# The first stage of layer 0 in a new order: vectors by rows, biases by columns, blocks finished pair by pair

## The chip, the cores and the metric

The kernel runs on one core of a Trainium2 chip. The metric is the time of one execution in device microseconds. The time before is the median of three runs, 1631.57 us (1629.46 to 1635.71).

## The reference, cut to what matters

One step of a trunk of two layers over 1024 latent tokens and 128 context tokens of width 1024, in float32. The change touches the start of layer 0: the modulation vectors, the pre-norm and the projection to keys and values.

```python
def adaln(cond, w, b):                       # w: 1024 x 3072
    m = (jax.nn.silu(cond) @ w + b)[:, None, :]
    return split_last(m, (D_MODEL, D_MODEL, D_MODEL))
def pre_norm(x, g, mod):
    shift, scale, _ = mod
    return rms_norm(x, g) * (1 + scale) + shift
...
for layer in range(DEPTH):
    mod_p = adaln(c_ctx[None, :], w_mod[layer], b_mod[layer])   # context tokens
    mod_s = adaln(c, w_mod[layer], b_mod[layer])                # latent tokens
    hp = pre_norm(xp, g_pre[layer], mod_p)
    hs = pre_norm(xs, g_pre[layer], mod_s)
    # layer 0: q, k, v, gates and the pooling input are columns of h @ w_in_e
```

## The kernel before

**Tokens and blocks.** The nine token tiles (eight latent, one context) of 128 x 1024 are `xn[t]`; group g is tiles 3g to 3g+2. Width 1024 is cut into eight blocks k of 128. `hTh[k]` and `hTl[k]` hold block k of the normed, scaled and shifted tokens, transposed, as a high part and a rest; weights are split in the same way into `whi` and `wlo`, and one product is three matmuls (high by high, high by rest, rest by high).

**The steps.** `norm_x(t)` squares and sums a tile on ACT (`sqx`), takes the root on ACT (`xd`), the reciprocal on DVE (`xr`) and scales the tile on DVE. `pn(k, g)` is `prenorm_k`: three transposes on PE into a PSUM tile `tp`, scale and shift on DVE into `hf` (two buffers), the high part on ACT (`hTh`), the rest on POOL (`hTl`, which frees `hf`). `kvg(k, ts)` does the nine matmuls per three token tiles that add block k to the key and value sums in five PSUM banks `acc`. A key and value chunk of 512 KB (`raw`) serves four blocks; `kv.split` makes its `whi` on ACT and its `wlo` on DVE.

**Modulation in quarters.** `mod_block(kp)` computes a quarter of shift and scale (two blocks k) for both conditions: 32 small matmuls of `wmb` (four loads of 512 KB) against `silrep`, the SiLU of the condition vectors spread over 32 rows; then `mrow` is written by DVE, and `mod_block_end` transposes it on PE and writes `sh` and `sc` on DVE. `pn(k, .)` needs quarter k // 2. `mod_ss(1)` does the same for layer 1 later, beside the query products.

**Order.** The program sets the order of every engine's instructions by hand; each engine and SP's queue, which issues all loads, works in that order. PE's order before: quarter 0, `pn(0..1, 0)`, the products of those, quarter 1, and from then on products of blocks prepared one or more steps earlier, between them the `pn` of later blocks and groups; group 2 follows late. Each quarter's end is issued after products of earlier blocks. Buffers: weights, squares and small tables share 17 tiles `w`; five PSUM banks `B` hold two of `acc`, the modulation and `tp`.

**Vectors before.** `c`, `c_ctx` and `g_pre` are loaded straight into columns (four bytes at a time), the bias `b_mod` of each quarter as rows spread over 32 partitions (`bm0`), added to `mrow`. Five matmuls of zeros open the sums in `acc` (L569).

**What follows.** At the end of the stage the first half of the query weights is split (`wl.need(0)`: twice `whi` on ACT, `wlo` on DVE), the rotary tables are scaled on POOL (`rtq`, `rtk`), and the query products (`qkv`) run beside the norm and transposition of the keys (`kv1` to `kv4`).

Of the kernel before, what the change touches and what calls it, by code (L numbers as in the profile page):

```python
# [19 lines left out]
EPS = 1e-6  # L20
# [35 lines left out]
class Kern:  # L56
# [87 lines left out]
    def setup0(self):  # L144
        nc, I = self.nc, self.I
        ct = self.K([128, 8, 2], name="ct")
        self.dma(ct[:, :, 0], I["c"][0].rearrange("(k p) -> p k", p=128))
        self.dma(ct[:, :, 1], I["c_ctx"].rearrange("(k p) -> p k", p=128))
        sl = self.K([128, 8, 2], name="sl")
        nc.scalar.activation(out=sl, in_=ct, func=AF.Silu)  # L150
        self.silrep = self.K([128, 8, 16, 2], name="silrep")
        self.vcopy(self.silrep, sl[:, :, None, :].to_broadcast([128, 8, 16, 2]))

    def setup(self):
        nc, I = self.nc, self.I
        self.ident = self.K([128, 128], name="ident")
        self.dma(self.ident, I["k_ident"])
        self.gpre = self.K([128, 2, 8], name="gpre")
        self.dma(self.gpre, I["g_pre"].rearrange("l (k p) -> p l k", p=128))
        self.eps = self.K([128, 1], name="eps")  # L160
        nc.vector.memset(self.eps, EPS)
        self.ones = self.K([128, 32], name="ones")
        nc.vector.memset(self.ones, 1.0)
# [19 lines left out]
    def mod_block_load(self, kp):  # L183

        r = []
        for i in range(2):
            for h in range(2):
                t = self.W([128, 4, 256], name="wmb")
                c = 1024 * i + 256 * kp
                self.dma(t, self.I["w_mod"][0, 512 * h:512 * h + 512, c:c + 256].rearrange("(k p) c -> p k c", p=128))  # L190
                r.append(t)
        return r

    def mod_block(self, kp, wt):

        ps = self.C("modps")
        for k in range(8):
            for j in range(4):
                self.mm(ps[32 * j:32 * j + 32, 0:128], self.sil(k),
                        wt[2 * (j // 2) + k // 4][:, k % 4, 128 * (j % 2):128 * (j % 2) + 128], k == 0, k == 7)  # L200
# [12 lines left out]
    def mod_ss(self, l):  # L213
# [18 lines left out]
        def fin():  # L232
            ps = box["ps"]
            bm = self.W([128, 512], name="bm")
            self.bcast_rows(bm, I["b_mod"][l], 512)
            mrow = self.W([128, 512], name="mrow")
            self.vtt(mrow, ps, bm, ALU.add)
            box["m"] = mrow

        def fin2():  # L240
            mrow = box["m"]
            ps2 = self.C("modT").rearrange("p (i q) -> p i q", i=4)
            for i in range(4):
                self.tr(ps2[:, i, :], mrow[:, 128 * i:128 * i + 128])
            v = ps2.rearrange("p i (j r) -> p i j r", j=4)
            self.vcopy(self.sh[l].rearrange("p (j i) s -> p i j s", j=2), v[:, :, 0:2, 0:2])
            self.vts(self.sc[l].rearrange("p (j i) s -> p i j s", j=2), v[:, :, 2:4, 0:2], 1.0, op0=ALU.add)
            self.vtt(self.sc[l], self.sc[l], self.gpre[:, l, :, None].to_broadcast([128, 8, 2]))
# [57 lines left out]
    def prenorm_k(self, l, g, k, xn, hi, lo, veng=False):  # L306

        b = self.B("tp")
        for i in range(3):
            self.tr(b[:, 128 * i:128 * i + 128], xn[i][:, 128 * k:128 * k + 128])  # L310
        hf = self.T([128, 384], tag="hf")
# [213 lines left out]
def layer0(kn):  # L525
# [18 lines left out]
    mb = {}  # L544
    mb[0] = kn.mod_block_load(0)
    load_x(0)
    kn.setup()
    kn.bm0 = kn.W([128, 4, 128], name="bm0")
    src = I["b_mod"][0]
    for j in range(4):  # L550
        kn.dma(kn.bm0[32 * j:32 * j + 32], bass.AP(tensor=src.tensor, offset=src.offset + 1024 * (j // 2) + 128 * (j % 2),
                                                   ap=[[0, 32], [256, 4], [1, 128]]))
    for t in range(1, 3):
        load_x(t)
    kv.load()
    for t in range(3, 6):
        load_x(t)
    mb[1] = kn.mod_block_load(1)
    for t in range(6, 9):
        load_x(t)  # L560

# [4 lines left out]

    zero = kn.W([128, 512], F32R, name="zero")
    nc.vector.memset(f32(zero), 0.0)
    for i in range(5):  # L569
        kn.mm(acc[i], zero[:, 0:128], zero, True, False)  # L570
# [4 lines left out]
    def pn(k, g):  # L575
        c = slice(384 * g, 384 * g + 384)
        kn.prenorm_k(0, g, k, xn[3 * g:3 * g + 3], hTh[k][:, c], hTl[k][:, c])
# [9 lines left out]
    kn.mod_block_end(*kn.mod_block(0, mb.pop(0)))  # L587
    for t in range(3):
        norm_x(t)
    pn(0, 0)  # L590
    mb[2] = kn.mod_block_load(2)
    pn(1, 0)
    kv.split(True)
    for t in range(3, 6):
        norm_x(t)
    for k in range(2):
        kvg(k, range(3))
    for k in range(2):
        pn(k, 1)
    m1 = kn.mod_block(1, mb.pop(1))  # L600
    mb[3] = kn.mod_block_load(3)
    kvg(0, range(3, 6))
    kn.mod_block_end(*m1)
    for k in range(2, 4):
        pn(k, 0)
    kvg(1, range(3, 6))
    for k in range(2, 4):
        pn(k, 1)
    for t in range(6, 9):
        norm_x(t)  # L610
    kvg(2, range(0, 6))
    m2 = kn.mod_block(2, mb.pop(2))
    kvg(3, range(0, 6))
    kn.mod_block_end(*m2)
    for k in range(2):
        pn(k, 2)
# [17 lines left out]
    wl._load(0)  # L634
    for k in range(2, 4):
        pn(k, 2)
    for k in range(4):
        pn(4 + k // 2, k % 2)
        kvg(k, range(6, 9))
    pn(4, 2)  # L640
    pn(5, 2)
    m3 = kn.mod_block(3, mb.pop(3))
    kvg(4, range(9))
    kn.mod_block_end(*m3)
    for g in range(3):
        pn(6, g)
    kvg(5, range(9))
    for g in range(3):
        pn(7, g)
    for c, w in rt.values():  # L650
        for i in range(2):
            kn.ptt(c[:, i], cs[:, i], w[:, i, None, :].to_broadcast([128, 8, 64]))
    wl.need(0)
    wl._load(1)
    kvg(6, range(9))
    kvg(7, range(9))
# [1642 lines left out]
```

## Time and profile before

| | us |
|---|---|
| median of three runs | 1631.57 |
| the profiled execution | 1633.59 |
| its span, first to last instruction | 1631.8 |
| PE busy, share of the span | 1542.5, 95% |
| mean granted clock of PE | 0.979 |
| start to the first key and value product | 25.09 |
| that product to the first query product | 47.88 |

The profiled execution is 2.0 us longer than the median, and 1.8 longer than its own span. PE's busy time is counted with the tails of pipelined matmuls. The page's lines by source often show one line for all matmuls (L97) or copies (L113, L118), since helpers issue them; the names of the tiles tell them apart.

### The profile page before, as it was taken

How to read it: one execution, taken by the hardware profiler on the slowest of the kernel's cores; microseconds unless marked ns; L12 is line 12 of the kernel's file. 1: busy time of each engine (PE TensorE's matmuls, PEld its weight loads, DVE VectorE, ACT ScalarE, POOL GpSimd, SP SyncE). 2: the span in 40 equal slices, each digit the busy share in tenths (PEclk: the TensorE clock that was granted, in tenths of full speed). 3: DMA queues.
4: the chain of work that ended last, by engine and by line, in shares of the span. 5: the costliest groups of instructions: out<-in, count | busy, mean ns of one | idle time of the engine just before them, and what ended most of it. 6: DMA issues, size and time to landing. Idle time of an engine off the chain costs nothing.

```text
span 1631.8 us, 23732 instructions
## 1 busy us (share of the span) xinstructions
PE 1542.5 (95%) x9132; PEld 1232.0 (76%) x9132; DVE 847.1 (52%) x1838; ACT 649.9 (40%) x1370; POOL 610.4 (37%) x485
## 2 busy tenths in 40 slices
PE   5989999999899999999999999999999999999998
PEld 4978998945455588898989898999865566655686
DVE  3574333347767555534354444424775665657633
ACT  4431211255455433445454544443453343444311
POOL 1643212058658423641303113001155454546421
PEclk7999999999999999999999999999999999999999
DMA  9443104120001132410404131040000000013341
GB/s 304 127 175 100 40 27 143 38 104 14 1 13 40 65 104 78 86 36 14 96 16 80 31 74 38 20 146 9 15 4 25 9 26 15 20 46 96 110 143 52
DMA packets 118805, 105.33 MB, mean 65 GB/s; under 512 B 45924, under 2 KB 104548, under 8 KB 118692
## 3 DMA queue, kind: packets, MB, share of 16 engines
q1 hardware_dynamic: 118692, 103.81, 21.5%
q8 instruction: 72, 1.18, 0.3%
q14 instruction: 41, 0.34, 0.1%
HBM read 88.05 MB, written 15.75 MB: 64 GB/s over the span
## 4 chain that ended last, share of the span: by engine, by line
PE 78%; DVE 8%; ACT 3%; POOL 2%; issue 1%; DMA 0%; SPq 0%; DVEq 0%; POOLq 0%; ACTq 0%
PE cg L97 15%; PE yps L97 11%; PE st L97 9%; PE gate L97 8%; PE pv L97 8%; PE mp L97 5%; PE lat L97 4%; PE cpv L97 3%; PE cS L97 2%; PE cT L106 2%; PE dq L97 2%; PE qkv L97 2%; DVE ms L131 1%; DVE mx L933 1%; PE dk L97 1%
## 5 line engine op out<-in xcount | busy, mean ns | idle before, releaser
L124 POOL TENSOR_TENSOR acc<-acc,P 128x1024 f32<-128x1024 f32 x98 | 233.3, 2381 | 109.9 <-ACT P L969 106.3
L969 ACT ACTIVATE P<-st 128x512 f32<-128x512 f32 x288 | 167.7, 597 | 189.8 <-PE st L97 170.7
L933 DVE TENSOR_REDUCE mx<-mp 128x1 f32<-128x384 f32 x384 | 193.1, 549 | 93.6 <-PE mp L97 91.0
L124 POOL TENSOR_TENSOR wlo<-raw,whi 128x1024 fp32r<-128x1024 f32 x36 | 87.3, 2427 | 275.6 <-ACT whi L113 220.0
L97 PE MATMUL yps<-whi,ohl 128*128 128x512 f32 x576 | 183.4, 393 | 0.0
L97 PE MATMUL cg<-hT1h,whi 128*128 128x384 f32 x480 | 170.9, 356 | 1.8 <-DVE hf L133 1.2
L97 PE MATMUL cg<-hT1h,wlo 128*128 128x384 f32 x480 | 163.8, 341 | 1.9 <-POOL wlo L124 1.9
L97 PE MATMUL cg<-hT1l,whi 128*128 128x384 f32 x480 | 163.4, 340 | 0.0
L97 PEld LDWEIGHTS yps<-whi,ohl 128*128 128x128 f32 x576 | 108.2, 188 | 26.0 <-issue 2.4
L97 PE MATMUL yps<-wlo,ohl 128*128 128x512 f32 x288 | 112.2, 390 | 0.0
L97 PE MATMUL gate<-hTh,whi 128*128 128x384 f32 x288 | 98.8, 343 | 4.8 <-ACT whi L113 4.8
L97 PE MATMUL gate<-hTh,wlo 128*128 128x384 f32 x288 | 97.5, 339 | 1.3 <-DVE wlo L121 1.3
L97 PE MATMUL gate<-hTl,whi 128*128 128x384 f32 x288 | 97.3, 338 | 0.0
L97 PEld LDWEIGHTS cg<-hT1h,whi 128*128 128x128 f32 x480 | 91.6, 191 | 6.6 <-issue 3.3
L97 PEld LDWEIGHTS cg<-hT1h,wlo 128*128 128x128 f32 x480 | 91.5, 191 | 2.2 <-POOL wlo L124 2.2
L97 PEld LDWEIGHTS cg<-hT1l,whi 128*128 128x128 f32 x480 | 91.7, 191 | 0.5
L1541 ACT ACTIVATE cs<-cs,cnm 128x640 f32<-128x640 f32 (+1 forms) x64 | 54.8, 857 | 92.0 <-DVE cnm L131 91.1
L97 PE MATMUL pv<-P,dV 128*64 128x512 f32 x288 | 80.0, 636 | 0.0
L97 PE MATMUL pv<-P,V 128*64 128x512 f32 x288 | 79.2, 628 | 0.0
L113 ACT CAST whi<-raw 128x1024 fp32r<-128x1024 f32 (+2 forms) x60 | 61.8, 1038 | 22.5 <-DMA raw<-in_w_in_e 8.7
L124 POOL TENSOR_TENSOR acc<-P 128x1024 f32<-128x1024 f32 x14 | 33.4, 2382 | 92.5 <-ACT P L969 91.9
L97 PEld LDWEIGHTS mp<-KH,QP 128*128 128x128 f32 x192 | 33.7, 190 | 41.7 <-DVE mx L933 14.7
(417 smaller groups left out, 3563.8 us busy)
## 6 DMA issues: line engine op xcount, KB each, us to landing
raw<-in_w_in_o SPq DMA_DIRECT2D x20, 512.0 KB, 4.0
raw<-in_w_in_e SPq DMA_DIRECT2D x18, 512.0 KB, 6.9
wmb<-in_w_mod SPq DMA_DIRECT2D x16, 512.0 KB, 9.1
wm<-in_w_mod SPq DMA_DIRECT2D x16, 512.0 KB, 5.5
wg<-in_w_mod SPq DMA_DIRECT2D x16, 512.0 KB, 4.0
x<-xr SPq DMA_DIRECT2D x9, 512.0 KB, 2.6
xr<-x SPq DMA_DIRECT2D x9, 512.0 KB, 3.9
xn<-in_x_sample SPq DMA_DIRECT2D x8, 512.0 KB, 8.0
```

The source lines that it names most:

```text
L97: self.nc.tensor.matmul(out=out, lhsT=l, rhs=r, start=st, stop=sp)
L106: self.nc.tensor.transpose(out, in_, self.ident[0:n, 0:n])
L113: self.nc.scalar.copy(out=out, in_=in_)
L124: self.nc.gpsimd.tensor_tensor(out=out, in0=a, in1=b, op=op)
L131: self.nc.vector.tensor_scalar(out=out, in0=a, scalar1=s1, scalar2=None, op0=op0)
L933: kn.nc.vector.tensor_reduce(out=self.mx[:, h, t, c:c + 1], in_=b, axis=AX.X, op=ALU.max)
L969: kn.nc.scalar.activation(out=P[:, h], in_=a, func=AF.Exp, scale=self.scale)
L1541: nc.scalar.activation(out=s[:, 0:n], in_=s[:, 0:n], func=AF.Exp, bias=nm, accum_out=sm)
```

## The change

- **Vectors.** `c`, `c_ctx`, `g_pre` and both layers' shift and scale biases are loaded as 64 rows of 128 by five transfers, and the identity by one, all six issued from ACT's queue ahead of ACT's other work. One transpose on PE turns the rows into columns; SiLU reads the PSUM tile, one DVE copy keeps the rest, and 1 is added to the scale biases once. `eps` and `ones` are set by POOL.
- **Biases.** `mrow` becomes a copy, and the biases are added to the columns at the end. For layer 1 the load of broadcast bias rows goes, the copy of `mrow` is on ACT.
- **Loads.** SP begins with x tiles 0 to 2, then quarter 0, the first half of the key and value weights, x 3 to 5, the second half, x 6 to 8, quarter 1. Quarters are loaded in the order in which their halves are used.
- **Zeros.** 25 matmuls of zeros instead of five before quarter 0, and five more behind its end.
- **Order.** Pairs of blocks are finished one after the other: for each group g the products `kvg(k, g)` alternate with `pn(k, g + 1)`; the next quarter's block stands between groups 1 and 2, its end behind group 2, and then the next pair's `pn(k, 0)`.

```diff
     def setup0(self):
...
+        self.ident = self.K([128, 128], name="ident")
+        nc.scalar.dma_start(out=self.ident, in_=I["k_ident"])
+        rows = self.rows = self.T([64, 128], tag="rows", bufs=1)
+        rv = lambda a: a.rearrange("(k p) -> k p", p=128)
+        for r, a in ((0, I["c"][0]), (8, I["c_ctx"]), (32, I["b_mod"][0, 0:2048]), (48, I["b_mod"][1, 0:2048])):
+            nc.scalar.dma_start(out=rows[r:r + a.shape[0] // 128], in_=rv(a))
+        nc.scalar.dma_start(out=rows[16:32], in_=I["g_pre"].rearrange("l (k p) -> (l k) p", p=128))
+
+    def setup(self):
+        nc = self.nc
+        b = self.B("col")[:, 0:64]
+        self.tr(b, self.rows)
+        sl = self.T([128, 2, 8], tag="sl", bufs=1)
+        nc.scalar.activation(out=sl, in_=b[:, 0:16].rearrange("p (s k) -> p s k", s=2), func=AF.Silu)
         self.silrep = self.K([128, 8, 16, 2], name="silrep")
+        self.vcopy(self.silrep, sl.rearrange("p s k -> p k s")[:, :, None, :].to_broadcast([128, 8, 16, 2]))
+        cols = self.K([128, 48], name="cols")
+        self.vcopy(cols, b[:, 16:64])
...
+        self.vts(self.bmc[:, :, 1], self.bmc[:, :, 1], 1.0, op0=ALU.add)
...
-        self.vtt(mrow, ps[:, 0:128], self.bm0[:, kp, :], ALU.add)
+        self.vcopy(mrow, ps[:, 0:128])
...
-        self.vcopy(self.sh[0][:, ks, :], v[:, 0:2, 0:2])
-        self.vts(self.sc[0][:, ks, :], v[:, 2:4, 0:2], 1.0, op0=ALU.add)
+        bc = lambda i: self.bmc[:, 0, i, ks, None].to_broadcast([128, 2, 2])
+        self.vtt(self.sh[0][:, ks, :], v[:, 0:2, 0:2], bc(0), ALU.add)
+        self.vtt(self.sc[0][:, ks, :], v[:, 2:4, 0:2], bc(1), ALU.add)
...
+    G = [range(3), range(3, 6), range(6, 9)]
+    zeros(10)
+    kn.setup()
+    zeros(10)
+    zeros(5, True, False)
+    m = kn.mod_block(0, mb.pop(0))
     for t in range(3):
         norm_x(t)
+    tps = [kn.prenorm_t(k, xn[0:3]) for k in range(2)]
+    kn.mod_block_end(*m)
+    zeros(5, False, False)
+    for k in range(2):
+        pn(k, 0, tps[k])
+    kv.split1(0, True)
     mb[2] = kn.mod_block_load(2)
+    for g in range(3):
+        if g < 2:
+            for t in G[g + 1]:
+                norm_x(t)
+        for k in range(2):
+            kvg(k, G[g])
+            if g < 2:
+                pn(k, g + 1)
+        if g == 0:
+            kv.split1(1, True)
+    m = kn.mod_block(1, mb.pop(1))
     mb[3] = kn.mod_block_load(3)
...
+    kn.mod_block_end(*m)
     for k in range(2, 4):
+        pn(k, 0)
+    for q in range(1, 4):
+        for g in range(3):
+            for k in range(2 * q, 2 * q + 2):
+                kvg(k, G[g])
+                if g < 2:
+                    pn(k, g + 1)
+            if g == 1 and q < 3:
+                m = kn.mod_block(q + 1, mb.pop(q + 1))
+            if g == 1 and q == 3:
...
+                wl.need(0)
+                wl._load(1)
+            if g == 2 and q < 3:
+                kn.mod_block_end(*m)
+                for k in range(2 * q + 2, 2 * q + 4):
+                    pn(k, 0)
```

More of the change, by code (lines that the diff above doesn't have):

```diff
@@ L145, in setup0 @@
         nc, I = self.nc, self.I
[L146 to L150, printed above, removed]
-        self.silrep = self.K([128, 8, 16, 2], name="silrep")
[L152 to L163, printed above, removed]
+        self.eps = self.K([128, 1], name="eps")
@@ L183, in mod_block_load @@
     def mod_block_load(self, kp):
[L185 to L188, printed above, removed]
+        r = {}
+        for h in range(2):
+            for i in range(2):
+                t = r[i, h] = self.W([128, 4, 256], name="wmb")
                 c = 1024 * i + 256 * kp
                 self.dma(t, self.I["w_mod"][0, 512 * h:512 * h + 512, c:c + 256].rearrange("(k p) c -> p k c", p=128))
-                r.append(t)
         return r
@@ L233, in fin @@
             ps = box["ps"]
-            bm = self.W([128, 512], name="bm")
-            self.bcast_rows(bm, I["b_mod"][l], 512)
             mrow = self.W([128, 512], name="mrow")
-            self.vtt(mrow, ps, bm, ALU.add)
+            self.acopy(mrow, ps)
             box["m"] = mrow
@@ L245, in fin2 @@
             v = ps2.rearrange("p i (j r) -> p i j r", j=4)
-            self.vcopy(self.sh[l].rearrange("p (j i) s -> p i j s", j=2), v[:, :, 0:2, 0:2])
-            self.vts(self.sc[l].rearrange("p (j i) s -> p i j s", j=2), v[:, :, 2:4, 0:2], 1.0, op0=ALU.add)
+            for x, (d, j) in enumerate(((self.sh, 0), (self.sc, 2))):
+                bc = self.bmc[:, l, x].rearrange("p (j i) -> p i j", j=2)[:, :, :, None].to_broadcast([128, 4, 2, 2])
+                self.vtt(d[l].rearrange("p (j i) s -> p i j s", j=2), v[:, :, j:j + 2, 0:2], bc, ALU.add)
             self.vtt(self.sc[l], self.sc[l], self.gpre[:, l, :, None].to_broadcast([128, 8, 2]))
@@ L310, in prenorm_k @@
             self.tr(b[:, 128 * i:128 * i + 128], xn[i][:, 128 * k:128 * k + 128])
+        return b
+    def prenorm_k(self, l, g, k, xn, hi, lo, veng=False, b=None):
+        if b is None:
+            b = self.prenorm_t(k, xn)
         hf = self.T([128, 384], tag="hf")
@@ L544, in layer0 @@
     mb = {}
+    for t in range(3):
+        load_x(t)
     mb[0] = kn.mod_block_load(0)
[L546 to L555, printed above, removed]
+    kv.load1(0)
     for t in range(3, 6):
         load_x(t)
-    mb[1] = kn.mod_block_load(1)
+    kv.load1(1)
     for t in range(6, 9):
         load_x(t)
+    mb[1] = kn.mod_block_load(1)
     hTh = [kn.S([128, 1152], F32R, name=f"hTh{k}") for k in range(8)]
@@ L568, in layer0, with zeros, pn @@
     nc.vector.memset(f32(zero), 0.0)
-    for i in range(5):
-        kn.mm(acc[i], zero[:, 0:128], zero, True, False)
+    def zeros(n, st=True, sp=True):
+        for i in range(n):
+            kn.mm(acc[i % 5], zero[:, 0:128], zero, st, sp)
     def kvps(t):
         return acc[t // 2][:, 256 * (t % 2):256 * (t % 2) + 256]
-    def pn(k, g):
+    def pn(k, g, b=None):
         c = slice(384 * g, 384 * g + 384)
-        kn.prenorm_k(0, g, k, xn[3 * g:3 * g + 3], hTh[k][:, c], hTl[k][:, c])
+        kn.prenorm_k(0, g, k, xn[3 * g:3 * g + 3], hTh[k][:, c], hTl[k][:, c], b=b)
     def kvg(k, ts):
@@ L634, in layer0 @@
     wl._load(0)
+    kn.mod_block_end(*m)
     for k in range(2, 4):
[L636 to L656, printed above, removed]
+        pn(k, 0)
[8 more added lines that the diff above has]
+            if g == 1 and q == 3:
+                for c, w in rt.values():
+                    for i in range(2):
+                        kn.ptt(c[:, i], cs[:, i], w[:, i, None, :].to_broadcast([128, 8, 64]))
+                wl.need(0)
[4 more added lines that the diff above has]
+                    pn(k, 0)
     p1.__exit__(None, None, None)
```

35 lines of the change are left out of this document (7 added, 28 removed).

## The prediction

> **What bounds the kernel now.** I read the page's span first, then a table of stretches, then the timeline of the stretch that the change touches, then the waits behind it.
>
> ```profile
> span 1631.8 us, 23732 instructions
> ```
>
> The change rewrites what lies between the start and the first query product. These rows give that stage in three parts, and three short stretches beside them; the columns are the stretch, its length, the busy time of PE, PEld, DVE, ACT and POOL, the granted clock, the share of the DMA engines and GB/s.
>
> ```profile
> 0.00:25.09 25.09, 8.80 (x77) 5.67 (x77) 5.51 (x17) 9.03 (x16) 1.78 (x6) 0.81 0.87 266
> 25.09:46.14 21.05, 18.88 (x219) 16.59 (x220) 12.83 (x25) 12.00 (x25) 6.32 (x7) 0.82 1.08 361
> 46.14:72.97 26.83, 25.69 (x259) 24.35 (x259) 15.18 (x33) 10.39 (x19) 17.92 (x17) 1.00 0.45 124
> ```
> ```profile
> 5.00:10.00 5.00, 3.56 (x21) 2.14 (x25) 0.83 (x4) 0.34 (x2) 0.00 (x0) 1.00 1.10 362
> 16.00:32.00 16.00, 8.41 (x31) 6.29 (x31) 10.23 (x21) 9.71 (x19) 1.96 (x2) 0.50 1.06 375
> ...
> 91.00:94.00 3.00, 3.00 (x16) 3.00 (x15) 1.38 (x6) 0.32 (x2) 2.18 (x4) 0.50 0.00 0
> ```
>
> Up to 25.09 us PE has little to do: the first quarter of the modulation waits for its bias rows and its transposed result for the norms. Then PE is 90% busy, at half clock until about 32 us; from 46.14 it is 96% busy (25.69 of 26.83) at full clock. So the last part is bound by PE itself, and only the first 25 us and the half clock are there to be won. Whatever makes the last part wait is a loss.
>
> ```profile
> 1.87 2.47 SPq L109 DMA_DIRECT2D wmb<-in_w_mod  x4
> ...
> 3.84 1.28 ACT L150 ACT_TABLE_LOAD   x1 [3.84 <-DMA ct<-in_c_ctx]
> ...
> 5.38 0.29 DVE L118 COPY silrep<-sl 128x256 f32<-128x256 f32 x1 [5.38 <-ACT sl L150]
> ...
> 16.56 0.29 DVE L121 TENSOR_TENSOR mrow<-modps,bm 128x128 f32<-128x128 f32 x1 [10.30 <-DMA bm<-in_b_mod]
> ...
> 20.90 0.75 DVE L131 TENSOR_SCALAR xn<-xn,xr 128x1024 f32<-128x1024 f32 x1
> ...
> 23.99 1.99 ACT L113 CAST whi<-raw 128x1024 fp32r<-128x1024 f32 x2
> ...
> 25.09 0.58 PE L97 MATMUL kv<-whi,hTh 128*128 128x256 f32 x1 [2.26 <-ACT whi L113]
> ```
>
> **The front, up to the first product.** The bias rows leave the path: the add at 16.56, which sat 10.30 us for them, becomes a copy. What binds next is the weights of quarter 0. Three x tiles and four weight tiles, 3.67 MB, now go first; SP's first issue moves from the small vectors to x, data runs from about 2.2 us (before, the weights issued at 1.87 were flowing by 4), and at 362 GB/s the last lands at 12.3. The rest of the block and the copy: 13.4. DVE is in order, so the reciprocals and scalings of the three norms stand behind that copy: 3 x 0.92 = 2.8, 16.2. Transposes, scale and shift, two hf (0.68 each), two hTh and the first whi (1.0, half of the pair of 1.99) on ACT follow: the first product at 20.6 instead of 25.09. That is a gain of 4.5 us.
>
> **The first section (blocks k = 0 and 1).** Order on each engine decides here. ACT gets three norms right behind that whi, and PE's transposes for group 1 stand ahead of kvg(1, group 0).
>
> ```profile
> 40.69 1.05 ACT L302 ACTIVATE sqx<-xn 128x1024 f32<-128x1024 f32 x1
> ...
> 42.07 1.04 ACT L302 ACTIVATE sqx<-xn 128x1024 f32<-128x1024 f32 x1
> ...
> 45.13 0.75 DVE L131 TENSOR_SCALAR xn<-xn,xr 128x1024 f32<-128x1024 f32 x1
> ```
>
> A norm takes 42.07 - 40.69 = 1.38 of ACT, three take 4.1, and the last xn ends 1.05 after that (45.88, against a last square that began at 43.45 and would be over with 1.38 at 44.83). So x 3 to 5 are ready at 20.6 + 4.1 + 1.05 = 25.7; PE, which ran kvg(0, group 0) by 23, waits 2.7. Then nine products 1.1 and the transposes, the hTh of (1, group 1) at 28.6, whi of the second half 29.6, three more norms 33.8, their xn 34.8, kvg(1, group 1) until 35.9, the chain of (1, group 2) to its hTl 3.1, seven products 0.85: 39.9. Quarter 1 of the modulation (1.9) follows bare, its copy and transpose (0.4) too: 42.2.
>
> **The steady part.** Now each pair of blocks is finished alone: kvg and pn alternate, and the next pair's first transposes come only after the modulation that scales them. These rows price the two chains that PE then meets.
>
> ```profile
> 41.97 1.96 PE L97 MATMUL modps<-wmb,silrep 128*32 128x128 f32 x64
> ...
> 46.14 0.33 PE L106 MATMUL modps<-ident,mrow 128*128 128x128 f32 x1
> ...
> 46.91 1.63 DVE L133 TENSOR_SCALAR hf<-tp,sc,sh 128x256 f32<-128x256 f32 x4
> ...
> 47.80 0.51 ACT L113 CAST hTh<-hf 128x384 fp32r<-128x384 f32 x1 [2.90 <-DVE hf L133]
> ...
> 48.39 1.97 POOL L124 TENSOR_TENSOR hTl<-hf,hTh 128x384 fp32r<-128x384 f32 x2 [6.51 <-ACT hTh L113]
> ...
> 57.90 0.39 PE L97 MATMUL kv<-whi,hTh 128*128 128x256 f32 x1
> ...
> 61.21 0.27 PE L106 MATMUL modps<-ident,mrow 128*128 128x128 f32 x1
> ```
> ```profile
> 65.52 1.14 PE L106 MATMUL tp<-ident,xn 128*128 128x128 f32 x9
> ...
> 66.12 0.68 DVE L133 TENSOR_SCALAR hf<-tp,sc,sh 128x384 f32<-128x384 f32 x1 [0.83 <-PE tp L106]
> ...
> 66.83 0.51 ACT L113 CAST hTh<-hf 128x384 fp32r<-128x384 f32 x1 [0.99 <-DVE hf L133]
> ...
> 67.42 1.99 POOL L124 TENSOR_TENSOR hTl<-hf,hTh 128x384 fp32r<-128x384 f32 x2 [0.50 <-ACT hTh L113]
> ```
>
> Twenty-seven products took 61.21 - 57.90 = 3.31, so nine take 1.1; three transposes take about 0.27 (the nine of 65.52 have 0.1 between starts). *Boundary chain*: from the transpose of mrow to hf 46.91 - 46.14 = 0.77, hf 0.68, hTh 0.05 + 0.51, product 0.06: 2.07; the third product also wants hTl, 1.07 later. *Inner chain*: from the first transpose to the end of hTl 68.42 - 65.52 = 2.9. PE has 0.27 + 1.1 + 0.27 + 0.24 = 1.9 of work to lay over it: it waits 1.1 for each pair's group 1. For group 2 the modulation block (1.9) covers it. One pair then takes 1.92 (first kvg with its hTl) + 0.27 + 1.1 + 0.27 + 2.2 + 0.27 + 1.1 + 0.27 + 1.9 + 2.2 + 2.07 = 13.6, of which PE's own work is 10.2. Before, these waits lay under kvg of blocks already prepared.
>
> The first pair of this kind begins at 42.2 + 2.07 = 44.3, the next at 57.9, the last at 71.5. It has 7.4 until its last transposes have ended, and 1.75 more until ACT is through hTh and begins whi of the query weights: 80.6.
>
> ```profile
> 69.79 2.00 ACT L113 CAST whi<-raw 128x1024 fp32r<-128x1024 f32 x2
> ...
> 72.97 0.28 PE L97 MATMUL qkv<-whi,hTh 128*128 128x256 f32 x1
> ...
> 76.78 0.41 DVE L502 TENSOR_REDUCE hss<-sq 128x4 f32<-128x256 f32 x1
> ...
> 89.67 0.66 PE L106 MATMUL kT<-ident,kh 128*128 128x128 f32 x4 [4.17 <-ACT kh L113]
> ```
>
> Before, that whi began at 69.79. Behind it the same chain stands in the same order (wlo, two casts, hss at 76.78, the key norms, kh), and PE waits 4.17 for kh at 89.67 whatever it has done meanwhile; so all that follows moves by 80.6 - 69.8 = 10.8 us.
>
> **The clock.** The products of zeros cover PE to about 12 us; then come the sparse transposes, five zeros, and gaps of 2.7 us at 23 and about 2.9 at 32. The rows show 0.50 from 16 to 32 with PE 53% busy, and 0.50 for 3 us after a wait of 4.17.
>
> ```profile
> 6.32 2.50 PE L97 MATMUL kv<-zero 128*128 128x512 f32 x5 [6.32 <-DVE zero L568]
> ...
> 27.21 0.41 PE L97 MATMUL kv<-whi,hTh 128*128 128x256 f32 x1
> ...
> 27.42 0.41 PE L97 MATMUL kv<-wlo,hTh 128*128 128x256 f32 x1
> ```
>
> At half clock products start 0.21 apart, so nine take 1.9, and three transposes about 0.6: 1.1 to 1.2 more for each kvg with its pn. From below nothing, if the zeros carry the clock through; from above four such steps, 4.8, if it stays half to 42. I take 1.1, one step, since the section leaves PE about as thinly used as 16:32. The Trainium skill (TensorE: Matmul & The Clock Gate, "Why this matters for your kernels") asks for no idle gap above some 3 us once PE has been busy for 4; by it both gaps just pass and the clock would be full, and the sum 10.8 instead of 11.9. The trace agrees as far as its one gap of 4.17 goes, at 0.50 after it; it has no gap of just under 3 us behind a busy stretch.
>
> **The other edits.** Six issues go to ACT's queue, where nothing went before.
>
> ```profile
> xn<-in_x_prompt SPq DMA_DIRECT2D x1, 512.0 KB, 10.2
> bm<-in_b_mod SPq DMA_DIRECT2D x4, 64.0 KB, 2.3
> ```
>
> At SP's 0.62 each (2.47 for four) the last is out at 4.5. It lands 2.3 us later at best, 10.2 at worst as the transfer behind a full queue did: 6.8 to 14.7. From landing to silrep took 5.67 - 3.84 = 1.83, with a transpose of 0.5 more: 9.1 to 17. At 9.1 it is hidden by the weights (first pair at 9.3); at 17 the block of 1.9 ends at 19 instead of 12.9, 6 us later. I take the first, nearest to the small transfers, since this is another queue. The Trainium skill (DMA: Bandwidth & Descriptors, "Issuing engines are not separate DMA queues") says that DMAs of different issuers interleave on the same 16 engines; by it small rows don't stand behind all of x, which lowers the chance of the late case. No run here shows a second queue. The 25 zeros ahead of the block cost nothing unless they outlast the weights: five took 2.50 at half clock, the tail of the last in it, so some 0.43 each; 25 from 1.4 end at 12.1, before 12.3. The five behind the transposes (2.1 at half clock) lie under the 3.5 from there to the first product. Memsets moved to POOL, which idles, cost nothing; biases added from columns replace a copy and a scaling by adds of the same few elements. In layer 1's modulation a transfer goes, a DVE add becomes an ACT copy while ACT idles, and fin2 keeps three small DVE ops, ahead of the last query norm:
>
> ```profile
> 149.76 0.72 DVE L121 TENSOR_TENSOR sc<-sc,gpre 128x16 f32<-128x16 f32 x1
> ```
>
> At worst the other two also take 0.72: 0 to 1.1; I take nothing. Loads of quarters 1 to 3 (three times 2.1 MB at 375 GB/s behind x) are in by 29, 35 and 41, before 40, 51 and 65 when they are used.
>
> Sum: -4.5 at the front, all of it lost again in the first section and the pairs, to +10.8, and +1.1 for the clock: +11.9 on the profiled execution of 1633.59, that is 1645.5; that execution stands 2.0 above the median of the three runs, 1631.57, so the median becomes 1643.5.
>
> **The rivals.**
> *Faster: PE stays dense.* Place: the inner and the boundary chain. If they were hidden as before, PE's own work (24 times 1.1 + 0.27, four blocks less one) of 39 us from 20.6 would end near 59.6, and whi begin 3.2 ahead of that end as before (72.97 - 69.79), at 56.4; half clock for the first three steps adds 3.5: 60, so -10, 1621.5. It decides at a chain of 1.9 instead of 2.9. For it: 96% from 46.14. Against: there each kvg ran over 6 to 9 tiles, here over 3, and hf has two buffers that only hTl frees.
> *Same: only the steady part is dense*, the first section's waits for norms remaining: 3 x 3.4 less than forecast, +1.7, 1633. It needs what DVE and ACT have queued to run ahead of PE by one step more than the program order gives.
> *Slower still: the vectors are late*, +6: 1649.5, with the point at silrep later than 9.3.
>
> **How the numbers follow.** Forecast 0.60, dense 0.10, same 0.20, late vectors 0.10. Half a per cent, 8.2 us, is about what a measurement of this kernel can tell from no change. Under 1623.4 lies the dense case, 0.10; between lie the same case and the lower edge of the forecast (clock full, chains 0.3 shorter), 0.27; above, 0.63. The range 1633 to 1651 leaves out the dense case and half of the tails, and takes in the forecast's 10.8 to 15.6 and the late vectors. The forecast's own: 1637 to 1648.
>
> **What would show it.** Right: mrow copied near 13.5, first kv product near 20.6, two PE gaps of some 2.7 us waiting for xn near 24 and 33, then PE near 75% with "kv <- ACT hTh" and "kv <- POOL hTl" among its longest waits, whi of the query weights past 78, and the stretches behind it unchanged but moved. Wrong: PE above 90% between 45 and 70, or query products before 75; or silrep after 10.

## The result, and the profile after

The change makes the kernel slower: 1654.84 us (median of four executions, 1651.76 to 1659.63) against 1633.21 for the kernel before (four, 1629.46 to 1635.71), a ratio of 1.0137 over all executions, here and below not that of the two medians (95% interval 1.0102 to 1.0172). The forecast was slower too, at 1643.5, with a range that ended at 1651. The profiled execution took 1651.76, its span is 1649.9; that is 18.1 us longer than the span before, where 11.9 were forecast. It is the shortest of the four, so the medians stand 21.6 apart; the three other spans, 1650.9 to 1657.8, go with a lower mean clock (0.971 to 0.974, against 0.977 here).

The table of stretches of the kernel after, cut at its own first product, at the transpose of quarter 1's `mrow`, and at the first query product. The columns are those of the prediction's tables.

```profile
0.00:23.96 23.96, 15.14 (x102) 10.24 (x102) 5.50 (x17) 8.77 (x16) 1.88 (x8) 0.92 0.89 316
23.96:48.63 24.67, 17.01 (x130) 14.84 (x130) 11.55 (x21) 10.98 (x23) 4.47 (x5) 0.66 0.87 276
48.63:90.30 41.67, 33.64 (x348) 29.66 (x348) 15.90 (x36) 11.32 (x21) 19.19 (x19) 1.00 0.25 71
```

Before, the first query product stood at 72.97; now at 90.30, 17.3 later. PE was 96% busy between 46.14 and that product; now it is 81% busy (33.64 of 41.67), at full clock, with more of the stage's work left to that part (348 matmuls on record instead of 259). The stretch between the first product and the transpose (24.67) has a mean clock of 0.66. Beside it the timeline, in the order of the prediction's steps:

```profile
0.75 4.95 SPq L109 DMA_DIRECT2D xn<-in_x_sample  x3
5.75 2.38 SPq L109 DMA_DIRECT2D wmb<-in_w_mod  x4
...
7.64 0.30 DVE L118 COPY silrep<-sl 128x256 f32<-128x256 f32 x1 [6.23 <-ACT sl L164]
...
15.67 1.07 PE L97 MATMUL modps<-wmb,silrep 128*32 128x128 f32 x28 [1.10 <-DMA wmb<-in_w_mod]
16.79 0.29 DVE L118 COPY mrow<-modps 128x128 f32<-128x128 f32 x1 [8.53 <-PE modps L97]
...
23.96 0.58 PE L97 MATMUL kv<-whi,hTh 128*128 128x256 f32 x1 [1.17 <-ACT whi L113]
...
29.07 0.48 PE L106 MATMUL tp<-ident,xn 128*128 128x128 f32 x1 [0.89 <-DVE xn L131]
...
36.80 0.33 PE L106 MATMUL tp<-ident,xn 128*128 128x128 f32 x1 [2.81 <-DVE xn L131]
...
46.24 1.96 PE L97 MATMUL modps<-wmb,silrep 128*32 128x128 f32 x64
48.63 0.33 PE L106 MATMUL modps<-ident,mrow 128*128 128x128 f32 x1 [0.44 <-DVE mrow L118]
...
88.09 1.99 ACT L113 CAST whi<-raw 128x1024 fp32r<-128x1024 f32 x2
```

And PE's waits between the first kv product and the first query product (us in total, times, longest):

```profile
PE tp L106 <- DVE xn L131: 5.6, 4, 2.8
PE kv L97 <- POOL hTl L124: 4.7, 8, 0.6
PE kv L97 <- ACT hTh L113: 3.8, 4, 1.2
```

The kinds of wait are those of the forecast: for xn in the first section, then for hTh and hTl, which stood at 0.2 and 1.0 before. Of its two gaps of 2.7 for xn the second came (2.81 at 36.80); the first shrank to 0.89 (at 29.07), since a wait of 1.02 for `wlo` and products at half clock filled it. What differs most is where the rows stand in time: the weights of quarter 0 release PE at 15.67 instead of 12.3, and the section behind the first product runs at half clock longer.

### The profile page after: what moved, and what is told of

It reads as the page before. It is cut to its first block, busy times and chain, and to the rows that moved or that the text cites. A ratio compares the mean times of both kernels' runs of the same rounds, so it can differ in the third digit from the quotient of the medians.

```text
span 1649.9 us, 23771 instructions
## 1 busy us (share of the span) xinstructions
PE 1556.6 (94%) x9158; PEld 1241.8 (75%) x9158; DVE 845.7 (51%) x1837; ACT 650.1 (39%) x1371; POOL 612.0 (37%) x487
## 4 chain that ended last, share of the span: by engine, by line
PE 77%; DVE 8%; ACT 3%; POOL 2%; issue 1%; DMA 1%; SPq 0%; DVEq 0%; POOLq 0%; ACTq 0%
PE cg L97 14%; PE yps L97 11%; PE st L97 9%; PE gate L97 8%; PE pv L97 7%; PE mp L97 5%; PE lat L97 4%; PE cpv L97 3%; PE cS L97 2%; PE cT L106 2%; PE dq L97 2%; PE qkv L97 2%; DVE ms L131 1%; DVE mx L938 1%; PE dk L97 1%
## 5 line engine op out<-in xcount | busy, mean ns | idle before, releaser
L97 PEld LDWEIGHTS cg<-hT1h,wlo 128*128 128x128 f32 x480 | 90.5, 189 | 2.2 <-POOL wlo L124 2.2
L97 PE MATMUL mp<-dKh,QH 96*128 96x384 f32 x192 | 61.4, 376 | 4.2 <-DVE mx L938 2.9
```

The costliest lines, as they stand in the source:

```text
L97: self.nc.tensor.matmul(out=out, lhsT=l, rhs=r, start=st, stop=sp)
```

## The experiments

Whole times of single executions differ by some us, so experiments are compared by the start of the first query product, and by whole times where there are several executions. Even the steady part, from the transpose of quarter 1's `mrow` to that product, differs between executions by up to 3 us (experiment 4), so a difference of 1 or 2 us in one execution shows little by itself.

**1. Order or front?** The kernel after with the compute order of before (the vectors by rows, the biases by columns and the new load order stay).

```diff
-    m = kn.mod_block(0, mb.pop(0))
-    ...                                     (the new order, group by group and pair by pair)
+    kn.mod_block_end(*kn.mod_block(0, mb.pop(0)))
+    ...                                     (the order of before, line for line)
```

> The changed kernel (vectors by rows, biases on columns, new loads, 25 zeros) with the compute order of before: quarter ends and transposes issued one or more steps ahead again. Theory 1 (the pair by pair order makes PE wait for the scale, cast and rest of each block): the first query product comes back from 90.3 us to 72 to 74, PE is above 93% busy in the 27 us ahead of it, and the time is that of before within 0.3%. Theory 2 (the vectors, loads and zeros of the front carry the loss): the first query product stays past 85 and the time stays over 1% above before.

Measured: 1633.67 against 1633.09 for the kernel before, ratio 0.9999 (0.9985 to 1.0014); query products from 72.4. PE in two stretches of 10 us:

```profile
50.00:60.00 10.00, 9.57 (x128) 8.97 (x128) 5.31 (x11) 3.83 (x8) 8.00 (x8) 1.00 0.86 238
60.00:70.00 10.00, 10.00 (x88) 10.00 (x88) 4.74 (x11) 3.77 (x7) 5.65 (x6) 1.00 0.19 57
```

The new order is the whole loss. But the first kv product stands at 23.0 here, 2 us before that of the kernel before, and the stage ends within 0.6 of where it did (72.4, 72.97): something takes the front's gain back (experiment 6).

**2. The order alone**: the kernel before with the new order of products, transposes and norms, and nothing else.

> The kernel before with the new compute order alone: vectors, biases, loads and five zeros stay as they were. Theory 1: first key and value product near 25, first query product at 89 to 92, time 1.0 to 1.3% above before. Theory 2: first query product within 3 us of 73 and the time of before.

Measured: 1652.74 (1650.65 to 1653.68), ratio 1.0112 (1.0087 to 1.0138); first kv product 26.4, query products from 92.6. The order without the new front costs as much as with it.

**3. The two chains.** The prediction's steady part says that the inner chain (1.1 per pair) and the boundary chain (2.07) lie bare. Two kernels lay them under products again, one chain each, and a third does both. The kernel for the boundary also moves the first section's modulation block, which lies bare in the kernel after, ahead of group 2's products; the lines below leave that out.

```diff
+            ks = range(2 * q, 2 * q + 2)            # inner
+            if g < 2:
+                for k in ks: pn(k, g + 1)
-            for k in range(2 * q, 2 * q + 2):
+            for k in ks:
                 kvg(k, G[g])
-                if g < 2: pn(k, g + 1)
+                if g == 2 and q < 3 and k == 2 * q:   # boundary
+                    kn.mod_block_end(*m)
+                    for j in range(2 * q + 2, 2 * q + 4): pn(j, 0)
-            if g == 2 and q < 3:
-                kn.mod_block_end(*m)
-                for k in range(2 * q + 2, 2 * q + 4): pn(k, 0)
```

> The changed kernel with one move in the steady part: for each pair of blocks from k = 2 on, both blocks' transposes of the next group are issued ahead of the products of the present group instead of after them. Theory (chains lie bare): each pair wins the wait of 1.1 that the prediction gave to its group 1, up to 2 where POOL's copy is waited for as well; three pairs, so the query products begin 3.3 to 6.5 us before 90.3 and the end moves by the same. Rival (DVE, ACT and POOL are full): the waits only change their place, and the query products stay within 1 us of 90.3.

> The changed kernel with one move at each boundary of two pairs: the transpose of mrow and the next pair's first transposes are issued between the two blocks' products of group 2 instead of after both; for the first pair the modulation block is moved ahead of group 2 as in the later pairs. Theory (chains lie bare): of each boundary's 2.07 us some 1.1 to 1.7 goes under products, and the first section loses its bare block of 1.96 and the copy behind it, 2 to 3 us: together the query products begin 4 to 7 us before 90.3. Rival (DVE, ACT and POOL are full): within 1 us of 90.3.

> Both moves of the two kernels before this one together. Theory (chains lie bare): the two gains add, 7.5 to 12 us, so the query products begin at 78 to 83 and the time is 1642 to 1647 against 1654.8 for the changed kernel. Rival (DVE, ACT and POOL are full): within 2 us of the changed kernel.

Measured, against 90.28: query products from 83.30 (inner, -7.0), 85.08 (boundary, -5.2) and 80.94 (both, -9.3). The block of quarter 0 ended at different times in these executions: mrow was copied 0.7 and 0.8 earlier than the 16.79 of the kernel after in the first two, 0.9 later in the third. If that passes on whole, the moves alone are worth 6.3, 4.4 and 10.2, and the two add up to the third within 0.6. In the boundary version the waits for hTh fall from 3.8 to 0.6. The third took 1642.76 (1640.52 to 1647.80; ratio to before 1.0063, 1.0041 to 1.0084). The same 40 us of the kernel after, of the boundary, the inner and the joint version, in that order:

```profile
50.00:90.00 40.00, 32.35 (x338) 28.61 (x339) 14.77 (x33) 11.02 (x21) 18.89 (x19) 1.00 0.25 74
```
```profile
50.00:90.00 40.00, 35.41 (x364) 31.61 (x363) 19.16 (x35) 10.37 (x19) 22.04 (x20) 1.00 0.26 74
```
```profile
50.00:90.00 40.00, 36.99 (x387) 34.13 (x388) 20.50 (x38) 12.27 (x24) 25.67 (x23) 1.00 0.26 74
```
```profile
50.00:90.00 40.00, 38.36 (x411) 36.67 (x411) 21.46 (x42) 13.04 (x27) 27.88 (x26) 1.00 0.27 75
```

PE goes from 81% to 96% of these 40 us, and DVE, ACT and POOL, which do more in them, stay below 70%: no engine but PE was full, the chains were bare. All four ran at full clock there. The inner move brought 2.1 per pair, not the 1.1 of the prediction. It also puts transposes under the wait for hTl that follows the boundary; how the 2.1 divides these runs don't separate. Part of the boundary version's gain is the first section's block, also not separated.

**4. The clock in the first section.** Thirty more products of zeros in its gaps, and nothing else moved.

> The changed kernel with 30 more matmuls of zeros in PE's gaps between quarter 0 and block 1 (5 ahead of the first transposes, 5 more behind the quarter's end, 10 ahead of each of the two waits for norms). If the half clock from about 20 to 44 us is what made the first section 3 us longer than predicted (24.7 us from the first product to the transpose of quarter 1 instead of 21.6), the granted clock stays at 1.0 there, nine products take 1.1 instead of 1.9, and the section takes 21 to 22. If zeros don't count for the clock, the clock stays at 0.5 and the section gets longer by up to 4 us, the zeros' own time.

Measured: query products from 90.0 instead of 90.3, time 1653.97 (one execution). From 20 to 35 us, with the zeros and in the kernel after without them:

```profile
20.00:35.00 15.00, 12.20 (x68) 9.79 (x68) 8.99 (x17) 9.88 (x19) 4.02 (x4) 1.00 1.08 363
```
```profile
20.00:35.00 15.00, 10.91 (x43) 8.82 (x41) 7.82 (x15) 8.57 (x16) 3.97 (x4) 0.54 1.07 364
```

The zeros hold the clock at 1.00 from 20 to 35, and the section takes 23.2 instead of 24.7, not the 21 to 22 that were expected (quarter 1's transpose at 47.11 instead of 48.63, the first product at 23.94 and 23.96). That is about one half-clock step of 1.1 to 1.2; half-speed products under the waits for xn had cost nothing, and others remain (mean clock 0.80 to 0.85 between 35 and 45). Of the 1.5, 1.2 came back in the steady part; the kernel after has the clock at 1.00 from 50 to 90, this execution has not:

```profile
80.00:90.00 10.00, 8.57 (x55) 7.75 (x54) 4.14 (x7) 4.09 (x7) 5.01 (x5) 0.85 0.01 2
```

This is no matter of the zeros. Eight of the profiled executions (the kernel after, and those of experiments 2, 4, 5 and 7) have the same order of work on PE in the steady part. In three (after, the order alone, the early split) it takes 41.5 to 41.7 at a mean clock of 1.00; in two (zeros, 15 and 10 zeros in experiment 5) 42.8 and 42.9 at 0.96; in the three others of experiment 5 44.4 to 44.5 at 0.92. With x first, for one, the clock falls in two places:

```profile
50.00:60.00 10.00, 8.09 (x50) 7.30 (x51) 2.96 (x6) 2.57 (x5) 4.15 (x5) 0.83 0.61 168
80.00:90.00 10.00, 8.42 (x51) 7.75 (x52) 2.91 (x6) 2.29 (x5) 5.03 (x5) 0.83 0.02 7
```

The same order on PE costs 0, 1.1 to 1.2 or 2.7 to 2.9 us more from one execution to the next. Why one execution falls and another doesn't, no run shows.

**5. Why the front was late.** First the loads of x 0 to 2 were written ahead of the vectors' loads in the program:

```diff
+    for t in range(3): load_x(t)
     kn.setup0()
-    for t in range(3): load_x(t)
```

> The changed kernel with the three first x loads ahead of the six vector loads in program order, nothing else. In the changed kernel SP issued the third x only at 5.4 us, after the identity from the other queue had landed, and the weights of quarter 0 came in up to 15.6 us instead of the predicted 12.3. If that wait is a turn of a fixed number of transfers in flight, it now falls on the last vector load, which waits for x tile 0 (about 4 us): third x issued before 2.5 us, last weights in at 12.5 to 13.5, modulation row copied at 13.7 to 14.7 instead of 16.79, first query product about 2.5 us earlier than 90.3. If the memory or the engines were simply slow at the start, nothing moves.

The hold stayed: SP's third x load still went out at 5.20, mrow was copied at 16.3, query products from 93.1 (the late end is the steady part's clock). The order of each engine's own instructions had not changed, so this run tells nothing of the cause. The program's instruction list does: every transfer of SP and ACT takes one of eight semaphores in turn, and the third x load, the ninth transfer, carries a wait for the first of them, the identity's. SP's own waits in the kernel after say the same:

```profile
SPq L109 <- DMA ident<-in_k_ident: 3.7, 1, 3.7
```

So next the identity went to POOL's queue and the two rows of `b_mod` became one transfer:

```diff
-        nc.scalar.dma_start(out=self.ident, in_=I["k_ident"])
+        nc.gpsimd.dma_start(out=self.ident, in_=I["k_ident"])
-        ... (32, I["b_mod"][0, 0:2048]), (48, I["b_mod"][1, 0:2048]) ...
+        nc.scalar.dma_start(out=rows[32:64], in_=bass.AP(tensor=bm.tensor, offset=bm.offset, ap=[[3072, 2], [128, 16], [1, 128]]))
```

> The changed kernel with two of its first eight transfers out of the way: the identity is loaded by POOL instead of ACT, and the two rows of b_mod by one transfer instead of two. In the changed kernel's instruction list each transfer of SP and ACT takes one of eight semaphores in turn, and the third x load waits for the first of them, which the identity holds until it has landed; here three x loads and the first weight load carry no such wait. Theory (the turn holds SP): the third x load goes out before 2.5 us instead of 5.37, mrow is copied at 13.3 to 14.5 instead of 16.79, the first product stands at 20.5 to 22 instead of 23.96, and the query products begin 1 to 3 us before 90.3. Rival (transfers, or ACT's queue, set it): mrow stays at 16 to 17. Second rival (POOL's transfer is slow): silrep later than 10 and mrow at 15 or later.

SP's third x load was out by 2.1 and its first weight load behind it; the turn then held the second weight load, for 2.3 us instead of 3.7 and with more bytes already under way. But mrow came at 17.0, query products from 93.1. The timeline of PE:

```profile
8.27 0.33 PE L106 MATMUL col<-ident,rows 64*128 64x64 f32 x1 [2.91 <-DMA rows<-in_g_pre]
8.54 6.51 PE L97 MATMUL kv<-zero 128*128 128x512 f32 x15
14.97 1.30 PE L97 MATMUL modps<-wmb,silrep 128*32 128x128 f32 x40
```

The vectors landed 1.1 later, behind more of x; PE stood idle until then, fell to half clock, and the 15 zeros behind the transpose took 6.51 and held the block. So the zeros are free only while what stands ahead of them is early. With 15 zeros ahead and 10 behind:

> The changed kernel with the identity loaded by POOL and the two rows of b_mod by one transfer, as in the kernel with that edit alone, and with 15 products of zeros ahead of the transposed vectors and 10 behind them instead of 10 and 15: there, the 15 behind ran at half clock until 14.97 and held the block that the weights had left free. Theory (the turn of the eight semaphores holds SP, 1.3 us of the 3.3 by which the front missed its forecast): the block waits for its last weights until 14.0 to 14.6, mrow is copied at 15.2 to 15.8 instead of 16.79, the first product stands at 22.3 to 23. Rival (weights land no earlier): mrow at 16.5 or later.

```profile
0.75 1.34 SPq L109 DMA_DIRECT2D xn<-in_x_sample  x3
2.13 3.92 SPq L109 DMA_DIRECT2D wmb<-in_w_mod  x4
...
14.42 1.07 PE L97 MATMUL modps<-wmb,silrep 128*32 128x128 f32 x28 [1.09 <-DMA wmb<-in_w_mod]
```

The last weights are in at 14.42 instead of 15.67, mrow is copied at 15.5, the first product stands at 23.09. The query products stay at 90.5: the first section took 24.7 as before, and the steady part 42.8 instead of 41.7, at a mean clock of 0.96. So the hold of SP is worth 1.25 at the weights in this pair of executions. Over all profiled ones it is less: where SP is held, the last of PE's waits for these weights ends between 14.78 and 15.84 (nine executions, mean 15.2); with the freed front and no late zeros, between 14.10 and 14.42 (four, mean 14.3). The hold is worth about 0.9, some 0.5 of the 15.67 belongs to that one execution, and about 2 of the forecast's error there are still open. Last, the six loads behind the weights were held back, by a small copy of POOL from a weight tile into the tile of the first of them:

```diff
+    def hold_tile(r):
+        nc.gpsimd.tensor_copy(out=r[:, 0, 0:4], in_=mb[0][0, 1][:, 0, 0:4])
+        return r
-    kv.load1(0)
+    kv.load1(0, lambda *a, **k: hold_tile(kn.W(*a, **k)))
```

> The kernel with the freed front and 15 and 10 zeros, and one small copy by POOL from an early weight tile of quarter 0 into the tile of the first kv weights, ahead of that tile's load: so SP holds this load and the five behind it until that weight tile is in, about 11 us instead of 8.05. Theory (loads issued behind the weights share the DMA engines with them: by 14.42 us 4.46 MB had moved, 0.69 more than x 0 to 2, the weights and the vectors hold): the last weights of quarter 0 land 0.8 to 1.8 us sooner, so the block's last wait ends at 12.6 to 13.6 instead of 14.42 and mrow is copied at 13.7 to 14.7 instead of 15.5; the stage as a whole may lose, since all later loads start later. Rival (the weights' own transfers take that long): the last wait ends at 14.1 or later.

```profile
13.14 0.37 SPq L109 DMA_DIRECT2D raw<-in_w_in_e  x1
...
14.26 1.07 PE L97 MATMUL modps<-wmb,silrep 128*32 128x128 f32 x28 [0.93 <-DMA wmb<-in_w_mod]
```
```profile
0.00:13.00 13.00, 10.28 (x60) 7.48 (x62) 1.07 (x4) 5.49 (x10) 1.13 (x8) 1.00 0.85 286
```

No load was issued between the weights and 13.14, and still the weights' last wait ends at 14.26, within the 14.10 to 14.42 of the freed front without the hold; the query products begin at 92.0. The theory of shared engines falls. By 13.00, a mean of 286 GB/s had moved 3.72 MB of the 3.77 that x 0 to 2, the weights and the vectors hold. The forecast reckoned bytes at 362 GB/s from 2.2 us on and took the last byte for the landing. Here the mean from 2 to 13 us is 333 (57 GB/s from 1 to 2, then (3.72 - 0.06) / 11); the rate stands near 354 until 12 and then runs out:

```profile
11.00:12.00 1.00, 1.00 (x25) 0.72 (x28) 0.00 (x0) 0.99 (x3) 0.00 (x0) 1.00 1.11 351
12.00:13.00 1.00, 0.58 (x18) 0.31 (x12) 0.00 (x0) 0.97 (x4) 0.06 (x1) 1.00 0.67 212
13.00:14.00 1.00, 0.33 (x4) 0.06 (x4) 0.00 (x0) 0.96 (x2) 0.12 (x1) 1.00 0.13 45
```

At 333 the 3.77 MB would end at 13.1, 0.8 after the forecast's 12.3. The other 1.2 until the release at 14.26 hold a thin tail of the last bytes (45 GB/s from 13 to 14) and what lies between the last byte and the release; how long each is these rows don't say.

**6. What takes the front's gain back in the order of before?** In experiment 1 PE waits for the weights of quarter 1, which the new load order puts behind x 6 to 8 (its waits from 20 to 45 us):

```profile
PE modps L97 <- DMA wmb<-in_w_mod: 1.4, 2, 1.1
```

```diff
     kv.load1(1)
+    mb[1] = kn.mod_block_load(1)
     for t in range(6, 9): load_x(t)
-    mb[1] = kn.mod_block_load(1)
```

> The changed kernel with the compute order of before (as in the first such kernel), and the weights of quarter 1 loaded ahead of x 6 to 8 again, as before, instead of behind them. Theory (the new load order takes back what the front wins): PE's waits of 2.5 us for those weights go, the query products begin at 70 to 71 instead of 72.4, and the time is 1 to 3 us below that of before, 1630 to 1632. Rival (something else, such as x 6 to 8, takes their place): the query products stay at 72 to 73 and the time within 1 us of before.

> The kernel with the compute order of before and the weights of quarter 1 ahead of x 6 to 8, and besides the identity by POOL, the b_mod rows by one transfer and 15 products of zeros ahead of the vectors, 10 behind. Theory (in this order the stage follows its weights): the query products begin 1 to 2.5 us before those of the kernel without these edits of the front, at 68 to 70. Rival (norms and casts set it): within 0.7 us.

Measured: with the weights of quarter 1 ahead of x again, query products from 70.9 instead of 72.4 though mrow came 0.6 later, no such wait between 20 and 45, time 1630.60 (12 executions, ratio to before 0.9992, 0.9977 to 1.0007). With the freed front too, 69.6, one execution of 1628.86.

**7. Does the split of the kv weights set the first section?** PE waits 1.02 for `wlo` behind its first product, and the prediction had left `wlo` out.

```diff
+    kv.split1(0, True)
     kn.mod_block_end(*m)
...
-    kv.split1(0, True)
```

> The changed kernel with one move: the first half of the kv weights is cast and split ahead of the end of quarter 0's block, so that wlo (1.56 us of DVE) is made before the two hf and the norms of x 3 to 5, not between them. Theory (the prediction left wlo out: PE waits 1.02 for it behind the first product, and the scalings of x 3 to 5 stand behind it): no wait for wlo, the nine products of the first kvg end at 25 to 26 instead of 27.43, the norms of x 3 to 5 end 0.5 to 1.5 us sooner, and quarter 1's transpose of mrow stands at 46.8 to 48 instead of 48.63. Rival (the norms and the half clock alone set this section): the transpose stays within 0.5 us of 48.63.

Measured: no wait for `wlo`, the first product at 22.18 and quarter 1's transpose at 47.30, 1.3 earlier. That lies in the range of the theory, but 0.8 of it is mrow's own, copied at 15.99. Counted from that copy the transpose comes 0.5 sooner. PE, free of `wlo`, now waits for each xn of x 3 to 5 instead of once for the last:

```profile
25.07 0.30 PE L106 MATMUL tp<-ident,xn 128*128 128x128 f32 x1 [0.85 <-DVE xn L131]
26.35 0.48 PE L106 MATMUL tp<-ident,xn 128*128 128x128 f32 x1 [0.97 <-DVE xn L131]
27.71 0.47 PE L106 MATMUL tp<-ident,xn 128*128 128x128 f32 x1 [0.89 <-DVE xn L131]
```

The norms, spaced some 1.37 apart by ACT, set this part of the section, and the wait for `wlo` lay under them. The 0.5 fits ACT: its first square of x 3 begins 6.5 after mrow's copy instead of 7.0, with the cast of `whi` no longer just ahead of it. So for the split of `wlo` the rival holds, as far as one execution shows.

**8. All of it together**, on the order of before: weights of quarter 1 ahead of x 6 to 8, the freed front, and

```diff
+    for t in range(3): norm_x(t)
     kn.mod_block_end(*kn.mod_block(0, mb.pop(0)))
-    for t in range(3): norm_x(t)
     pn(0, 0)
...
     pn(1, 0)
-    kv.split(True)
+    kv.split1(0, True)
     for t in range(3, 6): norm_x(t)
+    kv.split1(1, True)
```

> All that the runs point to: compute order of before, weights of quarter 1 ahead of x 6 to 8, identity by POOL, b_mod rows by one transfer, 15 and 10 zeros, the first three norms issued ahead of the block of quarter 0 (so that their scalings don't stand behind its copy on DVE), and the two halves of the kv weights cast apart, the second behind the norms of x 3 to 5. Theory: first kv product at 19.5 to 21.5, query products from 66 to 69, time 1626 to 1630, 0.997 of before. Rival (norms and casts on ACT set the stage whatever stands ahead): query products at 70 or later and the time within 2 us of before.

Measured: first kv product at 19.49, query products from 68.4, 4.6 before the kernel before. The whole time is 1630.03 (12 executions, 1625.24 to 1636.96) against 1631.77 (23): ratio 0.9983, 0.9967 to 1.0000. The stage is faster, by 4.6 in the profiled execution, whose span is 5.1 shorter (1626.7 and 1631.8). The medians differ by 1.7, or 0.2%, which this measurement just fails to tell from none: the executions of one kernel spread over some 10 us.

## Why the prediction was right in sign and short in size

Its terms on the profiled execution, each against the rows above:

| step of the prediction | forecast, us | measured | difference |
|---|---|---|---|
| start to the first kv product | 20.6 | 23.96 | +3.4 |
| first section, with the clock term | 21.6 + 1.1 | 24.67 | +2.0 |
| steady part, to the first query product | 83.8 - 42.2 = 41.6 | 41.67 | +0.1 |
| what follows | moves as one | 17.3 at the query products, 18.1 at the end | +0.8 |

Together 6.3 beside 18.1 - 11.9 = 6.2. (83.8 is the forecast's whi at 80.6 and the 3.18 from there to the first query product.) The median missed the forecast by 11.3: 6.2 are in these rows, 1.6 is the median of before (1633.21 with a fourth execution, 1631.57 in the forecast), and by 3.5 the medians stand further apart than the profiled spans. No other execution of this kernel has a profile; a steady part at half clock for some us (experiment 4) would give 1.1 to 2.9 of that last part, and fits their lower mean clock, but that is not shown.

- **Right in its waits, lucky in its sum: the steady part.** The waits are the ones named, and experiment 3 shows it by laying them under products again. The boundary chain holds: 2.15 from the transpose of mrow at 62.71 to the first product at 64.86, where 2.07 were forecast. But the 0.1 is made of errors that cancel. A pair took 14.0 instead of 13.6 (transposes of mrow at 48.63, 62.71 and 76.70), 0.8 too little for two; the rest, up to the query product, took 13.6 instead of 14.4, since that product followed whi by 2.2 and not by 3.18. PE's idle time was 41.67 - 33.64 = 8.0, where three pairs with 1.1 and 2.07 make 9.5. And the forecast put the clock of this part at full: that held in this execution and two others, and failed by 1.1 to 2.9 us in five (experiment 4).

```profile
62.71 0.27 PE L106 MATMUL modps<-ident,mrow 128*128 128x128 f32 x1
```
- **Right: all that follows moves.** The key transposes moved by 18.1 (89.67 to 107.82) with the wait for kh at 3.9 instead of 4.2.
- **Half right: biases, vectors and zeros cost nothing.** silrep at 7.64 was ready before the forecast's 9.1, and the block waits for its weights. That the zeros are free hangs on the vectors being early (experiment 5). But the six issues on ACT's queue did cost: they took the semaphores that held SP's third load.
- **Mis-sized: the front, -4.5 forecast, -1.1 measured** (25.09 to 23.96). From the copy of mrow to the first product it took 7.2 as forecast; the copy itself came 3.4 late. The failed step is "at 362 GB/s the last lands at 12.3": PE's wait for it ended at 15.67. SP's third load stood 3.7 us behind a semaphore that the identity held, worth 1.25 at the weights against one execution and 0.9 over all (experiment 5); the mean rate was lower, and bytes moved is not yet a landing. The Trainium skill (DMA: Bandwidth & Descriptors, "Anatomy of one DMA — SWDGE (gpsimd) path") states, of transfers that GpSimd issues, that the semaphore can't fire until the last byte is confirmed landed in the target memory. The loads here are SP's, and the trace agrees in kind: the release came at 14.26, with 3.72 of 3.77 MB over at 13.00. The Trainium skill (DMA: Bandwidth & Descriptors, "Issuing engines are not separate DMA queues") says that issuing on several engines at once only saves the time it takes to issue; here a second issuing engine cost SP a hold of 3.7 us, by the shared turn of the program's semaphores.
- **Mis-sized: the clock, +1.1 forecast, some 2.8 measured.** The failed step is "I take 1.1, one step". At half clock ran the products of two kvg on the path, from 29.2 to 31.8 and from 39.7 to 42.2, and a part of a third, some 2.5 steps of 1.1 to 1.2: 2.8, near the middle of the prediction's bounds of 0 to 4.8. Experiment 4 shows one such step; the rest is read from the rows. The rule of the Trainium skill that the prediction weighed (TensorE: Matmul & The Clock Gate, "Why this matters for your kernels": no idle gap above about 3 us) would have had the clock full; the trace shows that this is not enough. The longest wait between 15 and 20 us was 1.25, with PE busy 2.01 of 5.00, and between 20 and 25 the clock was 0.52. (The trace of before has a second long wait that the prediction left out: 4.21 ahead of 16.91, with 0.50 from 16 to 32 behind it.)

```profile
17.99 0.33 PE L106 MATMUL tp<-ident,xn 128*128 128x128 f32 x1 [1.25 <-DVE xn L131]
```
```profile
15.00:20.00 5.00, 2.01 (x33) 1.36 (x34) 2.76 (x7) 0.29 (x1) 0.00 (x0) 1.00 1.05 394
20.00:25.00 5.00, 3.37 (x11) 2.06 (x9) 2.71 (x6) 3.03 (x6) 1.97 (x2) 0.52 1.04 392
```
- **The rivals.** Dense did not come; experiments 1 and 3 show which order it takes. The late vectors did not come either. "Same" asked that the engines run ahead of PE by one step more than the program gives; they did not, and experiment 3 shows what it takes: the step has to be in the program, and then PE is at 96%. That kernel is still 0.6% above before. In its profile the first section is what is left: PE is busy there for 15.70 of 23.02, and behind it for 31.59 of 32.68.
- **Not settled:** why the clock falls in the steady part of some executions and not of others; how much of the spread of whole times, 8 us in four executions, that makes; and how the last 1.2 us ahead of the release in experiment 5 divide.

## What to carry to other kernels

Finishing blocks one by one bares every chain between engines: before such a reordering, lay each chain (transpose, scale, cast, rest) beside the products that are issued while it runs, in the order of the program; what isn't covered is the price. Here that sum named the right waits and missed a pair by 0.4 of 14. A PE laid so thin can also lose its clock, as it did in five of eight executions here, so allow for that too. A load's landing is not its bytes over the peak rate: look in the instruction list for what the issuing queue waits for, use the rate that the first microseconds of a trace show, and add the time from the last bytes to the release. And where a gain at the front vanishes, look for the next load that the new order has put later.

## What the hardware showed unexpectedly

- SP's third load stood still for 3.7 us while its first two were under way, and the DMA engines ran nearly dry behind it: 114 GB/s between 5 and 6 us, against 408 between 4 and 5 and 315 in the same microsecond when the hold was gone.

```profile
4.00:5.00 1.00, 1.00 (x3) 0.75 (x3) 0.00 (x0) 0.68 (x1) 0.00 (x0) 1.00 1.02 408
5.00:6.00 1.00, 1.00 (x3) 0.33 (x1) 0.00 (x0) 0.00 (x0) 0.00 (x0) 1.00 0.33 114
```

- The clock fell to half without a long gap: 40% of sparse work between 15 and 20 us, with no wait above 1.25, came ahead of it. From 16.74 on that work was transposes alone; whether their share or their kind counts, no run separates. Full speed from 20 to 35 us took zeros in every gap, and then bought 1.5 us, of which later half-clock steps took 1.2 back.
- At 81% busy, the same products in the same order kept the full clock in three executions and lost it for some us, once or twice, in five: 41.5 to 44.5 us for the same part.
